# First loads of x and of the first weight chunk: one DMA queue before, two after

## The chip, the cores and the metric

The kernel runs on one core of one Trainium2 chip. The metric is the device time of one execution in microseconds (us); the median of three runs before the change is 1243.56 us (1243.49 to 1244.97). The core has TensorE (PE, matrix products), VectorE (DVE), ScalarE (ACT), GpSimd (POOL) and SyncE (SP, which only issues transfers and waits). Each engine executes its own instructions strictly in the order in which the program lists them; engines wait for one another, and for transfers, by semaphores.

## The reference

One inference step of a four-layer decoder trunk in float32 on 288 rows of x (256 of a prompt, 8 x 4 of samples), 1024 columns wide. Each layer computes `x += mixer(rmsnorm(x)); x += sqReLU-MLP(rmsnorm(x))`. Layer 0, in which all of the change lies, has the gating mixer:

```
u, v = split(gelu(h @ w_in), 2)          # h = rmsnorm(x); w_in is 1024 x 2048
v    = rmsnorm(v, sgu_g)
out  = (u * (masked w_s @ v + b_s)) @ w_out
```

## The kernel before

**Layout.** x is held transposed: eight tiles `x[k]` of 128 x 288. A weight matrix comes in chunks of 128 x 2048 (1 MB); a chunk of `w_in` gives two output tiles, each a sum over k = 0 to 7. Every product is made of three PE passes with operands split in two parts: whi * xh, whi * xl, wlo * xh (function `mm3`, lines 283 to 285). So a chunk is 2 x 8 x 3 = 48 matmuls.

**Splitting.** For each k ACT writes `xh[k]` (line 294) and DVE `xl[k]` (line 295). For each chunk ACT writes `whi` (line 207) and DVE `wlo` (line 208), in two halves; for the first chunk, raw0, in four quarters of 512 columns. Quarter s holds the weights of k = 2s and 2s+1, and the first two quarters are split in `W.piece()`, the other two in a second call; ahead of quarter s the source asks for `xh`, `xl` of k = 2s and 2s+1 (function `first` near the end of `body`). The raw buffers and the split buffers are three deep.

**The norm.** ACT squares x[k] (lines 300 and 306), POOL adds the squares (line 307, seven additions), a matmul sums them over partitions (line 321), ACT takes the root (line 329), and DVE makes 1/root with a Newton step (lines 330, 311 to 314). Only then can DVE scale the first chunk's result out of PSUM (line 481), and PE, which has five accumulators, gets one back for its sixth output tile. At the start PE runs 14 warm-up products (line 337) that need no data.

**What sets the order.** The source is not the order of execution. At build time a list scheduler orders each engine's instructions by its own estimates and priorities; the hardware then keeps that order. The lists shown under the change are from the built programs. Transfers use eight hardware semaphores in turn (DMAHW0 to 7): the ninth transfer waits, on its issuing engine, until the first has landed, and so on.

**The first loads.** All are issued by SP: aux (80 KB of small vectors), x[0], quarter 0, x[1..3], quarter 1, x[4..7], quarters 2 and 3, then chunks 1 and 2 in two halves each, `ident`, and the constants of layer 0.

Of the kernel before, what the change touches and what calls it, by code (L numbers as in the profile page):

```python
# [161 lines left out]
class Weights:  # L162
# [7 lines left out]
        self.todo = []  # L170
        self.first = None

    def load(self, upto, parts=None):
        while self.n_dma < min(upto, len(self.srcs)):
            i = self.n_dma
            if i not in self.raw:
                self.raw[i] = self.rawp.tile([P, 2048], F32, tag='raw', name=f'raw{i}')
                self.todo += [(i, p) for p in range(2)]
            t = self.raw[i]
            n = 4 if i < 1 else 2 if i < 3 else 1  # L180
            w = 2048 // n
            a, b = parts or (0, n)
            for s in range(a, b):
                self.nc.sync.dma_start(t[:, s * w:(s + 1) * w], self.srcs[i][:, s * w:(s + 1) * w])
            if b < n:
                return
            self.n_dma += 1

    def piece(self):
# [34 lines left out]
def body(tc, a, o, layers=(0, 1, 2, 3)):  # L224
    nc = tc.nc
    V, S, G, PE = nc.vector, nc.scalar, nc.gpsimd, nc.tensor
# [11 lines left out]
    W = Weights(tc, srcs, rawp, hip, lop)  # L238
# [3 lines left out]
    xall = persist.tile([P, KT, T], F32, name='x')  # L242
    x = [xall[:, k] for k in range(KT)]
    nc.sync.dma_start(aux, a['aux'])
    nc.sync.dma_start(xall[:, 0:1], a['xT'][:, 0:1])
    W.load(1, parts=(0, 1))
    nc.sync.dma_start(xall[:, 1:4], a['xT'][:, 1:4])
    W.load(1, parts=(1, 2))
    nc.sync.dma_start(xall[:, 4:8], a['xT'][:, 4:8])
    W.load(1, parts=(2, 4))  # L250
    A = {n: aux[:, i] for i, n in enumerate(AUX)}
    ident = persist.tile([P, P], F32, name='ident')
    ones = persist.tile([P, P], F32, name='ones')
# [952 lines left out]
def program(inputs, layers=(0, 1, 2, 3)):  # L1206
    import concourse.bacc as bacc
    nc = bacc.Bacc("TRN2", target_bir_lowering=False, num_devices=1)
    arrays, a, o = {}, {}, {}
    for n, v in layout(inputs).items():  # L1210
        arrays[f"in_{n}"] = v
        a[n] = nc.dram_tensor(f"in_{n}", v.shape, mybir.dt.from_np(v.dtype), kind="ExternalInput").ap()
    for n, s in OUTS.items():
        o[n] = nc.dram_tensor(f"out_{n}", s, F32, kind="ExternalOutput").ap()
    with tile.TileContext(nc) as tc:
        body(tc, a, o, layers)
    return nc, arrays
# [7 lines left out]
```

## Time and profile before

| | us |
|---|---|
| median of 3 runs | 1243.56 |
| the profiled execution's own time | 1242.8 |
| its span (first to last instruction) | 1241.1 |
| PE busy | 1216.4 (98%) |
| DVE busy | 853.4 (69%) |
| ACT busy | 679.2 (55%) |
| mean granted TensorE clock | 0.997 of full speed |

A row of the timeline gives the start in us from the span's start, the duration, the engine, the source line, the operation, out<-in, the count of merged instructions, and in brackets the idle time before it with what ended that. SPq rows are SP issuing transfers. In a table by windows each row is a stretch, with the busy time of each engine in it, the granted clock, the share of DMA engines that are busy, and GB/s.

### The profile page before, as it was taken

The page shows a single profiled execution, that of the slowest core. Times are in us where ns is not written, and L with a number is a line of the kernel's source. Part 1 is how long each engine was busy: PE and PEld are TensorE (multiplying, and loading weights), DVE is VectorE, ACT ScalarE, POOL GpSimd, SP SyncE. Part 2 cuts the span into 40 slices and gives each one's busy share as a digit, 9 for nine tenths or more (in the row PEclk, how much of TensorE's full clock was granted, in tenths as well). Part 3 has the DMA queues.
Part 4 walks back from the last instruction along what each step waited for, and adds up shares of the span by engine and source line. Part 5 has one row for each costly group of instructions (what it writes and reads, how often), then busy time and mean ns, then how long its engine had stood idle before and what let it go on. Part 6 is the DMA issues. An engine that isn't in the chain of part 4 may idle for free.

```text
span 1241.1 us, 23859 instructions
## 1 busy us (share of the span) xinstructions
PE 1216.4 (98%) x9802; PEld 1198.6 (97%) x9802; DVE 853.4 (69%) x1485; ACT 679.2 (55%) x1159; POOL 144.8 (12%) x192
## 2 busy tenths in 40 slices
PE   8999999999989999999999999999999999999997
PEld 7999999999889999999998999999999999999997
DVE  5789986676789976787698556555566686554553
ACT  5757734754686753574433457436645557634641
POOL 4302000001432200001111210000013110000011
PEclk9999999999999999999999999999999999999999
DMA  8537565565425786676677344444445535554431
GB/s 306 182 133 240 179 218 171 196 203 191 148 73 205 234 263 209 209 239 211 206 289 266 112 169 162 164 158 167 166 171 196 174 137 170 170 170 162 160 120 39
DMA packets 56006, 227.70 MB, mean 183 GB/s; under 512 B 16649, under 2 KB 22201, under 8 KB 33369
## 3 DMA queue, kind: packets, MB, share of 16 engines
q1 hardware_dynamic: 54472, 221.83, 53.2%
q0 software_dynamic: 848, 3.75, 0.9%
q8 instruction: 77, 1.26, 0.4%
q10 hardware_dynamic: 576, 0.59, 0.1%
q14 instruction: 33, 0.26, 0.1%
HBM read 209.45 MB, written 16.70 MB: 182 GB/s over the span
## 4 chain that ended last, share of the span: by engine, by line
PE 88%; DVE 7%; DMA 2%; POOL 1%; ACT 1%; issue 1%; SPq 0%; DVEq 0%; ACTq 0%
PE acc L285 27%; PE acc L283 27%; PE acc L284 27%; DVE wlo L208 2%; PE sec L1054 1%; PE sec L532 1%; PE acc L1092 1%; PE acc L1096 1%; PE acc L1046 1%; DMA sco<-scr 1%; DMA x<-in_xT 1%; DMA bt<-in_bt 0%; DVE hl L280 0%; POOL eg L666 0%; DVE xc L635 0%
## 5 line engine op out<-in xcount | busy, mean ns | idle before, releaser
L207 ACT ACTIVATE whi<-raw 128x1024 fp32r<-128x1024 f32 (+1 forms) x354 | 364.1, 1049 | 386.0 <-PE acc L284 364.4
L208 DVE TENSOR_TENSOR wlo<-raw,whi 128x1024 fp32r<-128x1024 f32 (+1 forms) x354 | 426.2, 1222 | 128.7 <-ACT whi L207 126.7
L283 PE MATMUL acc<-xh,whi 128*128 128x288 f32 x1472 | 440.4, 299 | 3.9 <-DVE t L481 1.8
L285 PE MATMUL acc<-xh,wlo 128*128 128x288 f32 x1472 | 437.9, 298 | 5.9 <-DVE wlo L208 5.8
L284 PE MATMUL acc<-xl,whi 128*128 128x288 f32 x1472 | 431.8, 294 | 0.0
L283 PE MATMUL acc<-hh,whi 128*128 128x288 f32 x1024 | 303.3, 296 | 0.0
L284 PE MATMUL acc<-hl,whi 128*128 128x288 f32 x1024 | 302.4, 295 | 0.7 <-DVE hl L280 0.7
L285 PE MATMUL acc<-hh,wlo 128*128 128x288 f32 x1024 | 301.5, 294 | 0.0
L283 PEld LDWEIGHTS acc<-xh,whi 128*128 128x128 f32 x1472 | 277.3, 188 | 7.9 <-ACT whi L207 2.7
L285 PEld LDWEIGHTS acc<-xh,wlo 128*128 128x128 f32 x1472 | 276.4, 188 | 8.0 <-DVE wlo L208 7.3
L284 PEld LDWEIGHTS acc<-xl,whi 128*128 128x128 f32 x1472 | 280.6, 191 | 1.6 <-DVE xl L295 0.3
L284 PEld LDWEIGHTS acc<-hl,whi 128*128 128x128 f32 x1024 | 192.4, 188 | 1.1 <-DVE hl L280 0.9
L285 PEld LDWEIGHTS acc<-hh,wlo 128*128 128x128 f32 x1024 | 192.7, 188 | 0.2 <-issue 0.2
L283 PEld LDWEIGHTS acc<-hh,whi 128*128 128x128 f32 x1024 | 192.2, 188 | 0.2 <-issue 0.2
L307 POOL TENSOR_TENSOR ss<-ss,sq 128x288 f32<-128x288 f32 x62 | 69.9, 1127 | 915.7 <-ACT sq L306 914.9
L433 DVE TENSOR_TENSOR t<-acc,r 128x288 f32<-128x288 f32 x64 | 29.3, 457 | 139.9 <-PE acc L285 139.9
L280 DVE TENSOR_TENSOR hl<-t,hh 128x288 fp32r<-128x288 f32 x128 | 57.5, 451 | 35.6 <-ACT hh L279 35.6
L410 ACT ACTIVATE t<-acc 128x288 f32<-128x288 f32 x128 | 51.4, 402 | 23.8 <-PE acc L285 23.7
L279 ACT ACTIVATE hh<-t 128x288 fp32r<-128x288 f32 x128 | 56.9, 444 | 3.7
L295 DVE SCALAR_TENSOR_TENSOR xl<-x,aux,xh 128x288 fp32r<-128x288 f32 x64 | 51.5, 815 | 10.2 <-ACT xh L294 10.2
L416 ACT ACTIVATE t<-t 128x288 f32<-128x288 f32 x128 | 56.0, 437 | 2.3 <-DVE hl L280 0.5
L294 ACT ACTIVATE xh<-x,aux 128x288 fp32r<-128x288 f32 x64 | 33.3, 527 | 28.9 <-DVE x L1113 15.3
(334 smaller groups left out, 1246.5 us busy)
## 6 DMA issues: line engine op xcount, KB each, us to landing
raw<-in_wall SPq DMA_DIRECT2D x173, 1024.0 KB, 5.0
sci<-scr SPq DMA_DIRECT2D x8, 768.0 KB, 8.7
sco<-scr SPq DMA_DIRECT2D x8, 768.0 KB, 7.3
scr<-zero SPq DMA_DIRECT2D x16, 256.0 KB
scr<-cn SPq DMA_DIRECT2D x8, 512.0 KB, 8.5
raw<-in_wall SPq DMA_DIRECT2D x4, 512.0 KB
bt<-in_bt SPq DMA_DIRECT2D x8, 256.0 KB
scr<-tab SPq DMA_DIRECT2D x8, 256.0 KB, 5.5
```

The lines of the kernel that those rows point to most:

```text
L207: nc.scalar.activation(h[:, c], self.raw[i][:, c], AF.Copy)
L208: nc.vector.tensor_tensor(l[:, c], self.raw[i][:, c], h[:, c].bitcast(F32), op=OP.subtract)
L279: S.activation(h, src, AF.Copy)
L280: V.tensor_tensor(l, src, h.bitcast(F32), op=OP.subtract)
L283: PE.matmul(ps, wh, h, start=first, stop=False)
L284: PE.matmul(ps, wh, l, start=False, stop=False)
L285: state['mm'] = PE.matmul(ps, wl, h, start=False, stop=last)
L294: state['xh'] = S.activation(xh[k], x[k], AF.Copy, scale=A[g][:, k:k + 1])
L295: V.scalar_tensor_tensor(xl[k], x[k], A[g][:, k:k + 1], xh[k].bitcast(F32), op0=OP.mult, op1=OP.subtract)
L307: G.tensor_tensor(state['ss'], state['ss'], q, op=OP.add)
L410: i = S.activation(q, ps[:, :T], AF.Relu)
L416: S.activation(q2, q, AF.Square)
```

## The change

x is loaded in five pieces on SP (x[0], x[1], x[2..3], x[4..5], x[6..7]) with no weights between them, and the four quarters of raw0 are issued by ACT on its own queue, ahead of everything else that ACT does.

```
-    def load(self, upto, parts=None):
+    def load(self, upto, eng=None):
...
-            a, b = parts or (0, n)
-            for s in range(a, b):
-                self.nc.sync.dma_start(t[:, s * w:(s + 1) * w], self.srcs[i][:, s * w:(s + 1) * w])
-            if b < n:
-                return
+            for s in range(n):
+                (eng or self.nc.sync).dma_start(t[:, s * w:(s + 1) * w], self.srcs[i][:, s * w:(s + 1) * w])
             self.n_dma += 1
...
     nc.sync.dma_start(aux, a['aux'])
-    nc.sync.dma_start(xall[:, 0:1], a['xT'][:, 0:1])
-    W.load(1, parts=(0, 1))
-    nc.sync.dma_start(xall[:, 1:4], a['xT'][:, 1:4])
-    W.load(1, parts=(1, 2))
-    nc.sync.dma_start(xall[:, 4:8], a['xT'][:, 4:8])
-    W.load(1, parts=(2, 4))
+    for b, e in ((0, 1), (1, 2), (2, 4), (4, 6), (6, 8)):
+        nc.sync.dma_start(xall[:, b:e], a['xT'][:, b:e])
+    W.load(1, eng=S)
```

The built program moves more than these loads. First SP, from its first transfer; x of 128x576 are the three pairs x[2..3], x[4..5], x[6..7], raw_131 is chunk 1, and [waits ...] names the semaphore of an earlier transfer that must have landed. After:

```order
L241 DMA aux<-in_aux 128x160
L243 DMA x<-in_xT 128x288 x2
L243 DMA x<-in_xT 128x576
L243 DMA x<-in_xT 128x576 [waits DMAHW0_49]
L243 DMA x<-in_xT 128x576 [waits DMAHW1_49]
L183 DMA raw_131<-in_wall 128x1024 [waits DMAHW2_49]
L183 DMA raw_131<-in_wall 128x1024 [waits DMAHW3_49]
```

DMAHW0 is the semaphore of quarter 0 on ACT's queue, DMAHW1 that of aux: SP now issues x[4..5] only when quarter 0 has landed. Before, no x load had such a wait.

Then ACT, from its first instruction to the last `xh`. Before (xh_91 to xh_98 are k = 0 to 7; whi_151 is the first chunk):

```order
L1177 ACT_TABLE_LOAD
L1177 ACTIVATE one_127<-eps 128x1
L294 ACTIVATE xh_91<-x,aux 128x288
L207 ACTIVATE whi_151<-raw_79 128x512
L294 ACTIVATE xh_92<-x,aux 128x288
L294 ACTIVATE xh_93<-x,aux 128x288
L294 ACTIVATE xh_94<-x,aux 128x288
L207 ACTIVATE whi_151<-raw_79 128x512
L294 ACTIVATE xh_95<-x,aux 128x288
L294 ACTIVATE xh_96<-x,aux 128x288
L207 ACTIVATE whi_151<-raw_79 128x512
```

After (xh_93 to xh_100 are k = 0 to 7; whi_153 is the first chunk):

```order
L183 DMA raw_83<-in_wall 128x512 x4
L1171 ACT_TABLE_LOAD
L1171 ACTIVATE one_129<-eps 128x1
L288 ACTIVATE xh_93<-x,aux 128x288
L288 ACTIVATE xh_97<-x,aux 128x288
L288 ACTIVATE xh_94<-x,aux 128x288
L288 ACTIVATE xh_98<-x,aux 128x288
L204 ACTIVATE whi_153<-raw_83 128x512 x2
L288 ACTIVATE xh_95<-x,aux 128x288
L288 ACTIVATE xh_99<-x,aux 128x288
L288 ACTIVATE xh_96<-x,aux 128x288
L288 ACTIVATE xh_100<-x,aux 128x288
```

ACT's order in k was 0, 1, 2, 3, ... with a quarter between; it is now 0, 4, 1, 5, two quarters, 2, 6, 3, 7. By the offsets of their operands in the built program the two quarters are the third (k = 4, 5) and then the first (k = 0, 1). DVE's `xl` and `wlo` follow the same order. PE's order in k is unchanged: 0, 1, 2, ... 7.

The next rows of ACT, up to the root of the norm (rq). After (sq are the squares of k = 2 and on; whi_238, whi_294, whi_401 are chunks 1, 2, 3):

```order
L300 ACTIVATE sq_184<-x 128x288
L204 ACTIVATE whi_153<-raw_83 128x512
L300 ACTIVATE sq_187<-x 128x288
L300 ACTIVATE sq_190<-x 128x288
L204 ACTIVATE whi_153<-raw_83 128x512
L300 ACTIVATE sq_193<-x 128x288
L300 ACTIVATE sq_196<-x 128x288
L204 ACTIVATE whi_238<-raw_131 128x1024
```

The two rows of whi_153 are the fourth quarter (k = 6, 7) and, last, the second (k = 2, 3). Before, only one quarter, the fourth, stood at this place, between sq_182 and sq_185; the second came before any square.

Last, DVE at the Newton step of the norm (r and rq), up to the first scalings of PSUM (t<-acc). Before:

```order
L330 TENSOR_SCALAR ms_352<-sec_350 128x288
L311 RECIPROCAL r_353<-rq_354 128x288
L312 SCALAR_TENSOR_TENSOR rq_354<-ms_352,r_353 128x288
L313 TENSOR_TENSOR rq_354<-rq_354,r_353 128x288
L314 SCALAR_TENSOR_TENSOR r_353<-rq_354,r_353 128x288
L481 TENSOR_TENSOR t_361<-acc_242,r_353 128x288
L481 TENSOR_TENSOR t_373<-acc_243,r_353 128x288
```

After (wlo_402 is chunk 3, wlo_486 chunk 4):

```order
L305 RECIPROCAL r_355<-rq_356 128x288
L205 TENSOR_TENSOR wlo_402<-raw_234,whi_401 128x1024
L306 SCALAR_TENSOR_TENSOR rq_356<-ms_354,r_355 128x288
L205 TENSOR_TENSOR wlo_486<-raw_236,whi_485 128x1024
L307 TENSOR_TENSOR rq_356<-rq_356,r_355 128x288
L205 TENSOR_TENSOR wlo_486<-raw_236,whi_485 128x1024
L308 SCALAR_TENSOR_TENSOR r_355<-rq_356,r_355 128x288
L475 TENSOR_TENSOR t_363<-acc_244,r_355 128x288
```

Three half-chunk splits of chunks 3 and 4 now stand inside the Newton step; before, they stood behind the scalings. ACT's halves of the same chunks stand, likewise, around rq and ahead of the table load for GELU. The first difference is at the start and the last one in the middle of layer 0's mixer; behind it the lists of all engines are the same.

## Rows read from the trace of the kernel before

**Rows 1.** The page: chain that ended last by engine; the commonest DMA issue.

```profile
PE 88%; DVE 7%; DMA 2%; POOL 1%; ACT 1%; issue 1%; SPq 0%; DVEq 0%; ACTq 0%
...
raw<-in_wall SPq DMA_DIRECT2D x173, 1024.0 KB, 5.0
```

**Rows 2.** Windows: stretch, length, busy PE, PEld, DVE, ACT, POOL, clock, DMA, GB/s.

```profile
0.00:40.00 40.00, 34.03 (x226) 30.87 (x227) 24.55 (x44) 25.51 (x50) 17.76 (x21) 1.00 0.71 250
40.00:1229.00 1189.00, 1178.79 (x9542) 1164.93 (x9542) 823.47 (x1427) 652.90 (x1109) 127.08 (x171) 1.00 0.54 182
```

**Rows 3.** Timeline of SP's queue: when each transfer is issued.

```profile
1.71 0.43 SPq L184 DMA_DIRECT2D raw<-in_wall  x1
...
9.53 0.33 SPq L454 DMA_DIRECT2D wT<-in_wsT  x1
10.20 0.34 SPq L456 DMA_DIRECT2D wS<-in_wsS  x1
10.85 0.35 SPq L459 DMA_DIRECT2D bsb<-in_bsr  x1
```

**Rows 4.** Timeline of ACT, 5 to 16 us.

```profile
5.43 0.63 ACT L207 ACTIVATE whi<-raw 128x512 fp32r<-128x512 f32 x1 [0.83 <-DMA raw<-in_wall]
...
8.79 0.62 ACT L207 ACTIVATE whi<-raw 128x512 fp32r<-128x512 f32 x1
9.54 0.97 ACT L294 ACTIVATE xh<-x,aux 128x288 fp32r<-128x288 f32 x2
10.41 0.62 ACT L207 ACTIVATE whi<-raw 128x512 fp32r<-128x512 f32 x1
10.93 0.95 ACT L294 ACTIVATE xh<-x,aux 128x288 fp32r<-128x288 f32 x2
11.78 0.43 ACT L300 ACTIVATE ss<-x 128x288 f32<-128x288 f32 x1
12.12 0.77 ACT L306 ACTIVATE sq<-x 128x288 f32<-128x288 f32 x2
...
14.82 0.44 ACT L306 ACTIVATE sq<-x 128x288 f32<-128x288 f32 x1 [0.91 <-POOL ss L307]
15.17 1.04 ACT L207 ACTIVATE whi<-raw 128x1024 fp32r<-128x1024 f32 x1
```

**Rows 5.** Timeline of POOL: the seven additions of squares.

```profile
12.63 9.15 POOL L307 TENSOR_TENSOR ss<-ss,sq 128x288 f32<-128x288 f32 x7 [10.46 <-ACT sq L306]
```

**Rows 6.** Timeline of PE, 0 to 30 us.

```profile
1.13 4.76 PE L337 MATMUL sec<-ones 128*128 128x128 f32 x28 [1.13 <-DVE eps L256]
6.11 0.41 PE L283 MATMUL acc<-xh,whi 128*128 128x288 f32 x1 [0.22 <-ACT whi L207]
...
23.23 0.30 PE L283 MATMUL acc<-xh,whi 128*128 128x288 f32 x1
...
23.62 0.65 PE L321 MATMUL sec<-ss,ones 128*128 128x288 f32 x2
...
29.26 0.40 PE L283 MATMUL acc<-xh,whi 128*128 128x288 f32 x1 [1.82 <-DVE t L481]
```

**Rows 7.** Timeline of DVE and ACT at the norm, and a later half split.

```profile
24.31 0.50 ACT L329 ACTIVATE rq<-sec,eps 128x288 f32<-128x288 f32 x1 [3.66 <-PE sec L321]
...
24.84 0.46 DVE L330 TENSOR_SCALAR ms<-sec 128x288 f32<-128x288 f32 x1 [1.98 <-ACT rq L329]
...
34.05 1.22 DVE L208 TENSOR_TENSOR wlo<-raw,whi 128x1024 fp32r<-128x1024 f32 x1 [0.49 <-ACT whi L207]
```

**Rows 8.** PE around its longest idle time, in layer 1.

```profile
355.73 0.61 PE L285 MATMUL acc<-xh,wlo 128*128 128x288 f32 x1 [3.78 <-DVE wlo L208]
356.13 0.45 PE L283 MATMUL acc<-xh,whi 128*128 128x288 f32 x1
...
359.01 0.31 PE L283 MATMUL acc<-xh,whi 128*128 128x288 f32 x1
```

**Rows 9.** Window behind that idle time (columns as in rows 2).

```profile
357.00:358.00 1.00, 1.00 (x6) 1.00 (x5) 1.00 (x2) 1.00 (x2) 0.00 (x0) 0.50 0.33 123
```

## The prediction, put on record before the changed kernel ran

> **What bounds the kernel now.** I read the page's busy times and its chain first. PE is busy 98% of the span (the table above) and holds 88% of the chain [rows 1]: a change is worth what it does to PE's idle time. The windows say where that is [rows 2]: in the first 40 us PE is idle for 40.00 - 34.03 = 5.97 us, in the next 1189 us for 10.21 us. All that the change moves lies in the first 40 us.
>
> Next, the timeline of SP's queue, which gives landing times, since SP waits for an earlier transfer before it issues a later one [rows 3]: x[4..7] has landed at 9.5, quarter 2 (counting from 0) at 10.2, quarter 3 at 10.85 us. With the sizes in the queue's order (aux 80 KB, x[0] 144, quarter 256, x[1..3] 432, quarter 256, x[4..7] 576, two quarters of 256) that is a curve: 1744 KB at 9.5, 2000 at 10.2, 2256 at 10.85. Quarter 0 (480 KB) ends ACT's idle time at 5.43 [rows 4].
>
> Then ACT and PE side by side. ACT splits quarter 0 at 5.43 and PE starts at 6.11, just behind it; quarter 1 is split at 8.79 to 9.41 [rows 4, 6]. PE reaches the sum of the norm at 23.62 and, after its sixth output tile has waited for a PSUM bank, goes on at 29.26 [rows 6]. From there PE hardly waits. So two moments measure the start: 23.62 and 29.26.
>
> **The change, part by part.**
>
> *Issue.* Four issues move from SP to ACT, ahead of ACT's table load. One costs about 0.43 us on SP [rows 3]; at that price ACT is busy for 1.7 us longer. That lies wholly ahead of the wait below, which ends at 10.0, and costs nothing.
>
> *When x[4..5] lands.* This now counts because the order puts xh of k = 4 second in ACT's strict queue: everything ACT does, the first quarter included, stands behind it. x[4..5] is itself issued only when quarter 0 has landed. On SP's queue 656 KB stand ahead of it, and with its own 288 KB that makes 944 KB; ACT's queue brings 1024 KB beside them. No row here shows two loading queues at once, so I bound it. If SP's queue wins, 944 KB and quarter 0 have moved, 1200 KB, at 7.7 us (on the line from 480 KB at 5.4 to 1744 KB at 9.5); but then quarter 2, which ACT splits first, comes late. Both are needed, 944 + 768 = 1712 KB, so one of the two is not there before 9.4. If everything comes at once it is 10.85, and with one more issue 11.3. With equal shares 1888 to 1968 KB have moved, 10.0 us. I take 10.0, which is also near the rows for the same data.
>
> [...]
>
> *ACT's new order.* By rows 4, an xh takes 0.43 us (9.54 to 10.41 for two), a quarter 0.52 to the next instruction and 0.62 to its end, a square 0.34. From 10.0: xh of k = 4, 1, 5 (that of k = 0 is done earlier), quarter 2 at 11.3, quarter 0 at 11.8, ready at 12.4: PE starts at 12.5 instead of 6.11. Then xh of k = 2, 6, 3, 7 from 12.3, the first square at 14.05, the next at 14.4. The squares alternate between two buffers, so they wait for POOL. Before, POOL's first addition began 0.51 us after the start of the second square (12.12 to 12.63), and the square that waits for POOL came 2.19 us later, at 14.82 [rows 4, 5]. Now: 14.4 + 0.51 + 2.19 = 17.1 for the last square ahead of quarter 1, quarter 1 at 17.45, ready at 18.07. Quarter 3 fits in between. PE wants quarter 1 (k = 2 and 3) directly after quarter 0; with 12 of 48 matmuls done it stands until 18.1.
>
> *PE up to the sum of the norm.* From 18.1 there are 36 matmuls of the first chunk and 48 of the second, at 0.13 us (three in 23.23 to 23.62) [rows 6]: 10.9 us, and 0.3 for the wlo of quarter 1. Chunk 1's splits are done by about 22 to 24 and don't stop it, as they did before. The sum comes at 29.3, 5.7 later than 23.62.
>
> *The Newton step.* Before, rq began 0.69 after the sum, ms 0.53 after that, and PE went on 4.42 after ms [rows 6, 7]. Now three half splits of wlo stand among DVE's Newton instructions, 1.22 us each [rows 7]: 3.66 us. Their inputs are there: chunk 3 is issued when the last wlo of the first chunk is done, about 19, chunk 4 by about 24, and 1 MB lands 5.0 us after its issue [rows 1]. ACT's three halves and the table load end near 35 and lie beside this. So PE goes on at 29.3 + 0.69 + 0.53 + 4.42 + 3.66 = 38.6, against 29.26: 9.3 us later. What stalls longer than before is the sixth output tile, from 32.7 to 38.6.
>
> *What comes back.* Chunks 3 and 4 are split earlier, so DVE and ACT have less to do from 39 on. PE, though, had almost no idle time to give back there [rows 2]; I put it at nothing.
>
> *The clock.* [...] PE will now be idle from 5.9, the end of the warm-up products [rows 6], to 12.5, from about 14.5 to 18.1, and from 32.7 to 38.6. [...] I count 1.2 for the second, since 0.3 us of waiting covers part of it, and 1.0 for the third, where PE soon waits for GELU anyway: 2.2 us.
>
> **Sum.** 9.3 + 2.2 = 11.5 us. On the profiled execution's 1242.8 that is 1254.3; the median of the runs is 0.8 above that execution, so 1255.1.
>
> **The rivals.** A kernel within 0.2% (2.5 us) of before can't be told from no change.
>
> - *The clock stays up* (chance 0.16): the three idle times are not answered by the lower level. Against it speaks the 3.78 us of rows 8; for it, that the 1.82 us of rows 6 went unpunished and that work lies between the first two stretches. 1242.8 + 9.3 + 0.8 = 1252.9.
> - *The loads come better than by equal shares* (0.12): both x[4..5] and quarter 2 by 9.4, with quarter 2 last, which ACT then begins at 9.4 in place of 11.3: 1.9 us less, 1253.2.
> - *They come worse* (0.09): x[4..5] at 11.3, all else 1.3 later: 1256.4.
> - *The late start is given back later* (0.03, the other side): layer 1 and 2 hold most of the 10.21 us of PE's idle time behind 40 us [rows 2]. Were those waits for something that does not start later, such as work already ahead of PE, the delay would fill them: 1255.1 - 10.2 = 1244.9, no change. It decides from the point where DVE and ACT run ahead of PE by 3.8 us or more ahead of layer 1's waits. Against it: the orders there are the same, and the longest wait is for a DVE split, and DVE gets its work from PE's results.
> - *The order is no hindrance and the loads are simply earlier* (0.03): quarter 0 is no longer issued behind aux and x[0], which ended at 1.71 [rows 3], two issues of some 0.45 us each, so PE starts 0.9 us earlier: 1242.7 at 1243.6 for before, no change; with all of the 5.97 us of idle time in the first 40 us gone, 1237.6. ACT's queue and the wait on SP speak against it, since xh of k = 4 can't come before 7.7.
>
> [...]
>
> **How the numbers follow.** My forecast, 1255.1, has a chance of 0.57. The first two rivals reach down to 1252.9, and together, clock and loads, to 1251.0; the third to 1256.4, and with both clock terms at 1.4 to 1257.0. The range is 1251.0 to 1257.5. Slower by over 0.2% are all of these, 0.94; same 0.04; faster 0.02.
>
> **What would show it.** Right: PE's first matmul on real data near 12.5; a second idle time that ends near 18.1 with quarter 1's split; the sum of the norm near 30; the sixth tile's matmul with an idle time of some 6 us ahead of it, near 40; granted clock of 0.50 in stretches behind these. Wrong: a first matmul before 9, an ACT row of k = 4 that does not wait for its load, no split between DVE's Newton rows, or PE idle time behind 45 us that shrinks by several us.

## The result, and the profile after

The changed kernel takes 1253.8 us, median of 6 runs (1252.88 to 1254.97), against 1243.53 (1243.03 to 1244.97, 6 runs) beside it: ratio 1.0079 (95% interval 1.0068 to 1.0090), 10.3 us slower. Forecast were 1255.1 and a range of 1251.0 to 1257.5. The profiled execution took 1253.64 us, its span is 1251.9; before, 1242.8 and 1241.1.

The windows of the changed kernel, columns as in [rows 2]:

```profile
0.00:40.00 40.00, 27.31 (x151) 26.11 (x151) 22.97 (x34) 19.82 (x33) 12.24 (x17) 0.79 0.75 263
40.00:1229.00 1189.00, 1179.08 (x9534) 1164.69 (x9535) 825.47 (x1435) 656.93 (x1121) 127.75 (x173) 1.00 0.55 182
```

Behind 40 us PE is idle for 9.92 us, 10.21 before. The loss lies ahead: by 40 us PE has done 151 matmuls in place of 226, and its mean clock there is 0.79.

ACT's timeline at the start (start, duration, engine, line, operation; in brackets the idle time before it and what ended that), which answers to [rows 4]:

```profile
0.81 1.87 ACTq L183 DMA_DIRECT2D raw<-in_wall  x4
...
9.04 1.39 ACT L288 ACTIVATE xh<-x,aux 128x288 fp32r<-128x288 f32 x3 [2.94 <-DMA x<-in_xT]
10.34 1.13 ACT L204 ACTIVATE whi<-raw 128x512 fp32r<-128x512 f32 x2
...
16.10 0.44 ACT L300 ACTIVATE sq<-x 128x288 f32<-128x288 f32 x1 [0.91 <-POOL ss L301]
16.45 0.61 ACT L204 ACTIVATE whi<-raw 128x512 fp32r<-128x512 f32 x1
```

ACT stands until 9.04 for xh of k = 4. Quarters 2 and 0 come behind it in one row, and quarter 1, at 8.79 before, only at 16.45, behind a square that waits for POOL.

PE of the same execution, which answers to [rows 6]:

```profile
11.52 0.61 PE L277 MATMUL acc<-xh,whi 128*128 128x288 f32 x1 [4.52 <-ACT whi L204]
...
17.12 0.61 PE L277 MATMUL acc<-xh,whi 128*128 128x288 f32 x1 [2.35 <-ACT whi L204]
...
31.35 0.65 PE L315 MATMUL sec<-ss,ones 128*128 128x288 f32 x2
...
39.88 0.61 PE L277 MATMUL acc<-xh,whi 128*128 128x288 f32 x1 [4.69 <-DVE t L475]
```

Its first matmul on real data comes at 11.52 in place of 6.11, the sum of the norm at 31.35 in place of 23.62 (7.73 later), and PE goes on at 39.88 in place of 29.26 (10.62 later). DVE between the two last, which answers to [rows 7]:

```profile
32.57 0.46 DVE L324 TENSOR_SCALAR ms<-sec 128x288 f32<-128x288 f32 x1 [5.18 <-ACT rq L323]
32.94 1.94 DVE L305 RECIPROCAL r<-rq 128x288 f32<-128x288 f32 x1
34.80 1.16 DVE L205 TENSOR_TENSOR wlo<-raw,whi 128x1024 fp32r<-128x1024 f32 x1
35.88 0.45 DVE L306 SCALAR_TENSOR_TENSOR rq<-ms,r 128x288 f32<-128x288 f32 x1
36.24 1.22 DVE L205 TENSOR_TENSOR wlo<-raw,whi 128x1024 fp32r<-128x1024 f32 x1
37.38 0.45 DVE L307 TENSOR_TENSOR rq<-rq,r 128x288 f32<-128x288 f32 x1
37.75 1.22 DVE L205 TENSOR_TENSOR wlo<-raw,whi 128x1024 fp32r<-128x1024 f32 x1
38.88 0.46 DVE L308 SCALAR_TENSOR_TENSOR r<-rq,r 128x288 f32<-128x288 f32 x1
39.37 1.79 DVE L475 TENSOR_TENSOR t<-acc,r 128x288 f32<-128x288 f32 x4
```

The three half splits stand between the Newton instructions, none of which waits for anything but its turn. Last, the clock (third column from the end), which answers to [rows 9]:

```profile
11.00:23.00 12.00, 9.13 (x35) 8.46 (x36) 8.69 (x11) 10.02 (x19) 8.61 (x8) 0.50 0.97 360
23.00:24.00 1.00, 1.00 (x8) 1.00 (x8) 1.00 (x1) 0.00 (x0) 1.00 (x2) 0.78 0.62 98
...
42.00:43.00 1.00, 1.00 (x7) 0.88 (x5) 0.00 (x0) 0.39 (x2) 0.22 (x1) 0.50 1.04 442
```

PE's granted clock is 0.50 from its first matmul on real data until 23.4, and again for 4.0 us from 39.88 on.

When the loads land, from SP's queue, which answers to [rows 3]: it waits for quarter 2 before the first of these issues, and for quarter 3 before the second.

```profile
8.66 0.67 SPq L1173 DMA_DIRECT2D ident<-in_ident  x1
9.38 0.59 SPq L448 DMA_DIRECT2D wT<-in_wsT  x1
```

With x[4..5] there at 9.04 (ACT, above), 1968 KB have landed by 9.4; before it was 2000 KB at 10.2. On the line of [rows 3], 1968 KB belong to 10.1, so the bytes are there 0.7 earlier. Landing times differ between traces, but not by so much that this is lost: 1968 KB are there at 9.4 to 9.5 in the four traces with the new loads that show it, and at 10.1 to 10.8 in the four with the old ones.

### The profile page after: what moved, and what is told of

It reads as the page before. It is cut to its first block, busy times and chain, and to the rows that moved or that the text cites. A ratio compares the mean times of both kernels' runs of the same rounds, so it can differ in the third digit from the quotient of the medians.

```text
span 1251.9 us, 23861 instructions
## 1 busy us (share of the span) xinstructions
PE 1221.0 (98%) x9802; PEld 1204.5 (96%) x9802; DVE 854.8 (68%) x1485; ACT 679.5 (54%) x1159; POOL 141.6 (11%) x192
## 3 DMA queue, kind: packets, MB, share of 16 engines
HBM read 209.45 MB, written 16.70 MB: 181 GB/s over the span
## 4 chain that ended last, share of the span: by engine, by line
PE 88%; DVE 8%; POOL 1%; ACT 1%; DMA 1%; issue 1%; DVEq 0%; ACTq 0%
PE acc L279 27%; PE acc L277 27%; PE acc L278 27%; DVE wlo L205 2%; PE sec L1048 1%; PE acc L1086 1%; PE acc L1040 1%; PE sec L526 1%; PE acc L1090 1%; DVE hl L274 0%; POOL eg L660 0%; PE sec L487 0%; DVE xc L629 0%; PE sec L945 0%; ACT whi L204 0%
```

## The experiments

Theory A: the order that the list scheduler made of the new loads costs the time, the loads themselves nothing. Theory B: the loads on two queues cost a part themselves, for instance since x[0] lands later. Ratios are to runs of the kernel before beside each group of experiments, with 95% intervals. The new loads are a second queue and also x in five pieces in place of three; no run here separates these two.

**1. The new loads, the old order.** The start is written out in the order of the kernel before, each instruction of ACT and DVE chained to the one ahead of it (n = square, q = quarter, x = xh and xl):

```
-    W.piece()
-    W.piece()
-    with tc.issue_after(state['xh'].ins):
-        for k in range(KT):
-            norm_square(k)
+    order = 'x0 q0 x1 x2 x3 q1 x4 x5 q2 x6 x7 n0 n1 n2 q3 n3 n4 n5 n6 n7'.split()
+    for o_ in order:
...
```

> The loads of the changed kernel (x in five pieces on SP, quarters on ACT's queue), but ACT and DVE forced into the order of before at the start: k = 0, quarter 0, k = 1, 2, 3, quarter 1, k = 4, 5, quarter 2, k = 6, 7, three squares, quarter 3. The build puts no half split into the Newton step then. Theory A (the static order costs, not the loads): the first real matmul near 6.5 us, the sum of the norm near 23.5, time 1243.5, at most 1245. Rival B (two queues bring x and the quarters too late, whatever the order): x[4..5] still lands at 9.0 and the rest of the start stays behind it, time 1249 or more.

1248.97 us (1248.19 to 1249.98), ratio 1.0040 (1.0026 to 1.0055): by the time alone, theory B. The trace says otherwise. ACT's rows from quarter 2 on stand where they stood before, to 0.02 us (10.41; first half of chunk 1 at 15.18, before 15.17). But the scheduler had moved two other things: the sum of the norm forward into chunk 1, where PE waited 4.47 us for POOL at 23.82, and what is seen under experiment 5. The run did not isolate the loads.

**2. The old loads, the new order.** Same edit on the kernel before, with the changed kernel's order:

```
+    order = 'x0 x4 x1 x5 q2 q0 x2 x6 x3 x7 n0 n1 n2 q3 n3 n4 q1 n5 n6 n7'.split()
```

> The loads of the kernel before, all on SP, but ACT and DVE forced into the changed kernel's order at the start (k = 0, 4, 1, 5, quarters 2, 0, k = 2, 6, 3, 7, three squares, quarter 3, two squares, quarter 1); the build then gives the changed kernel's order everywhere else too, the three half splits inside the Newton step included. Theory A: x[4..7] lands at 9.5 instead of x[4..5] at 9.0, so all is half a us later than in the changed kernel: 1254.3. Rival B: near before, 1245.

1256.47 us (1256.03 to 1257.67), ratio 1.0099 (1.0084 to 1.0115). The build put four half splits into the Newton step, not three as I had written. The order alone costs more than the whole change: xh of k = 4 waits until 10.21, the first matmul comes at 12.70, PE goes on at 41.16. Given this order, xh of k = 4 starts 1.17 us earlier with the loads on two queues. Not all of that is the loads': x[4..7] landed 0.67 later in this trace (10.20) than in the trace of the kernel before (9.53), which has the same loads. And the fourth split, at about 1 us (experiments 3 and 6), is part of what the time is above that of the changed kernel.

**3. The changed kernel with the splits of chunks 3 and 4 behind the Newton step.**

```
+                if i in (3, 4):
+                    for j in self.after:
+                        stay.enter_context(self.tc.issue_after(j.ins))
```

Here `after` holds the last Newton instruction and the first two scalings.

> The changed kernel, with the half splits of chunks 3 and 4 forced on DVE behind the Newton step and the first two scalings; the order at the start is the changed kernel's. Theory A: the three splits, 1.2 us each, leave the path to the sixth output tile, PE goes on near 36.3 instead of 39.9, and its idle time shrinks from 4.7 to about 1.2 us, after which the clock need not fall: 1253.8 - 3.6 - 1.1 = 1249.1. If the splits only fill time in which DVE would wait anyway, 1253.8 stays; if they come back as a wait later (GELU and scalings behind them), 1251 to 1253.

1249.51 us (1248.92 to 1250.28), ratio 1.0042 (1.0027 to 1.0057), 4.3 less than the changed kernel (4.6 by the ratios to the runs beside each), as expected. DVE and PE of this run:

```profile
32.24 0.46 DVE L329 TENSOR_SCALAR ms<-sec 128x288 f32<-128x288 f32 x1 [5.99 <-ACT rq L328]
32.61 1.94 DVE L310 RECIPROCAL r<-rq 128x288 f32<-128x288 f32 x1
34.59 0.46 DVE L311 SCALAR_TENSOR_TENSOR rq<-ms,r 128x288 f32<-128x288 f32 x1
35.08 0.46 DVE L312 TENSOR_TENSOR rq<-rq,r 128x288 f32<-128x288 f32 x1
35.58 0.46 DVE L313 SCALAR_TENSOR_TENSOR r<-rq,r 128x288 f32<-128x288 f32 x1
36.14 0.82 DVE L481 TENSOR_TENSOR t<-acc,r 128x288 f32<-128x288 f32 x2
```

```profile
36.65 0.40 PE L282 MATMUL acc<-xh,whi 128*128 128x288 f32 x1 [1.79 <-DVE t L481]
```

From ms to t it takes 3.90 us, in the changed kernel 6.80: the three splits cost 2.90, or 0.97 each, not their duration of 1.16 to 1.22. A split starts 0.1 before the row ahead of it ends, and so does the Newton row behind it; two Newton rows that follow each other directly have a gap of 0.03 to 0.10. And PE, having waited 1.79, has its full clock behind the wait (1.00 from 36 to 38 us).

**4. The changed kernel with more products of ones**: 25 warm-up products in place of 14, and 9 ahead of quarter 1's first matmul.

```
-    warm_up(14)
+    warm_up(25)
...
+                n = {(0, 2, 0): 9}.get((c, k, m), 0) if late else 0
```

> The changed kernel with 25 instead of 14 warm-up products at the start and 9 more behind the products of k = 0 and 1, so that PE is not idle while it waits for quarter 0 and for quarter 1. Clock theory: the 84 matmuls behind quarter 1 run at 0.13 us instead of 0.24 for the first 26 of them, the sum of the norm comes at 28.5 instead of 31.35, time 1253.8 - 2.8 = 1251.0. If the clock does not matter to the path, 1253.8; if the added products end after the data have come, 1254 to 1255.

1252.67 us (1252.02 to 1253.17), ratio 1.0067 (1.0052 to 1.0082). The clock is 1.00 until 38 us. From quarter 1's first matmul to the sum of the norm it now takes 12.01 us (17.61 to 29.62), in the changed kernel 14.23: 2.2 us of it were the low clock. In these 12.01 PE stands 0.51 for the wlo of quarter 1 (at 18.91), a wait that the low clock had covered. PE goes on 1.73 earlier (38.15), with the low clock still behind it (0.50 from 39 to 41). At the first addition of the next norm 2.00 are gained, at POOL's last addition 1.23, and the median is 1.1 less; the intervals of the two ratios overlap, so a gain in time is not shown. It is less than expected (see experiment 11).

**5. Experiment 1 with the sum of the norm held behind chunk 1, and the splits of chunk 3 held behind the first two scalings.**

```
             if c == late and before:
-                before()
+                with tc.issue_after(state['mm'].ins):
+                    before()
```

> The two-queue loads of the changed kernel, with the start written in the order of the kernel before on ACT, DVE and PE: the squares' sum stays PE's 113th row behind the whole of chunk 1, and chunk 3 is split behind the first two scalings, so that no split stands in the Newton step. Theory A (only the order that the build sets costs time, the loads nothing): first matmul on real data near 6.8, sum of the norm at 23.6 to 24.0, PE goes on at 29.3 to 29.7, 1243.5 us, between 1242.8 and 1244.5. Theory B (the loads on two queues cost part of the 10 us themselves, and the 5 us of the first experiment were theirs): sum at 25 or later, 1247 us or more.

1247.59 us (1245.81 to 1248.64), ratio 1.0027 (1.0016 to 1.0038). Again not what theory A expects; the cause shows in PE's row ahead of chunk 1 and the windows behind:

```profile
18.50 0.61 PE L282 MATMUL acc<-xh,whi 128*128 128x288 f32 x1 [2.50 <-ACT whi L209]
```

```profile
18.00:19.00 1.00, 0.50 (x2) 0.50 (x3) 0.63 (x2) 0.65 (x2) 0.92 (x2) 0.50 1.01 387
24.00:25.00 1.00, 1.00 (x7) 1.00 (x7) 0.00 (x0) 0.00 (x0) 0.67 (x2) 0.62 0.99 401
```

The first half split of chunk 1 on ACT ends at 16.70, the second at 18.45 (17.41 + 1.04): PE waited for the second. The built program tells why. The half whose load signals DMAHW2 is the one PE needs first:

```
21 L209 ACTIVATE whi1_238<-raw1_131 128x1024 [waits DMAHW3_49]
24 L209 ACTIVATE whi1_238<-raw1_131 128x1024 [waits DMAHW2_49]
```

The scheduler had swapped the two halves. Experiments 1, 5 and 6 have this, and experiment 8 has it in chunk 2; the kernels before and after do not have it in chunk 1. The wait of 2.50 us (0.75 before) brought the low clock, from 18.5 until 24.8.

**6. Experiment 5 without holding the splits back**: the build then puts four half splits into the Newton step.

> As the kernel with the order held, except that four half splits of 1.16 us each stand between DVE's Newton instructions (one more than in the changed kernel) and the start is undisturbed. Theory A: the sum of the norm stays at 23.6 to 24.0, PE goes on 4 x 1.16 = 4.6 later, at 34.1 in place of 29.4, with a low clock of about 1.0 behind it: 5.6 us above the kernel with the order held, 1249.1 us. If the splits were covered by PE's work on other tiles (a rival), within 1 us of it. Theory B makes no difference here beyond its own offset.

1250.80 us (1250.62 to 1252.03), ratio 1.0061 (1.0048 to 1.0075), 3.2 more than experiment 5 where 5.6 were expected. From the sum to PE's going on it is 9.55 us (26.84 to 36.39) against 5.63: 3.92 for four splits, again 0.98 each. The times are closer than that since experiment 5's own sum came 1.17 later (28.01), and its clock fell behind the wait too (0.50 from 36 to 38).

**7. The old loads in a better order**: quarter 3 split ahead of the squares, the first half of chunk 1 ahead of the fourth. The sum of the norm is held behind chunk 1, as in experiment 5.

```
+    order = 'x0 q0 x1 x2 x3 q1 x4 x5 q2 x6 x7 q3'.split()
```

> Loads of the kernel before; ACT splits quarter 3 ahead of the first square and the first half of chunk 1 ahead of the fourth square. PE's waits of 0.75 and 0.62 us ahead of chunk 1 should go, 1.4 us, if POOL's additions, which end about 0.45 later than 21.78, are still done when PE comes to the sum at 22.2: 1242.2 us, between 1241.5 and 1243.5. If POOL now ends last, 1243.0.

1242.77 us (1240.73 to 1244.26, 11 runs), ratio 0.9991 (0.9982 to 1.0000). PE goes on at 27.61 in place of 29.26, but its clock behind the same wait (1.81 us, before 1.82) is the low one here (0.50 from 28 to 31): of 1.65 us 0.15 is left at the first addition of the next norm (84.08 against 84.23), and 0.60 at POOL's last addition. The interval of the ratio reaches up to no gain.

**8. The new loads in that order.**

> The better order of the kernel beside it with the two-queue loads, chunk 3 split on DVE between the second and third scaling. Theory A: the same as that kernel within 0.5 us, 1242.5 us, since the loads are not what PE waits for once the order is the same. Theory B: above it by 3 us or more.

1243.12 us (1242.05 to 1245.02, 11 runs), ratio 0.9996 (0.9987 to 1.0004): no difference to experiment 7 that can be told. The build slipped something in again: on POOL two mask operations among the squares' additions (rows under experiment 10), so that PE waited 2.11 us for POOL ahead of the sum.

**9. Experiment 5 with the halves of chunks 1 and 2 held in order.**

```
+                if p and i in (1, 2):
+                    for j in self.prev[i]:
+                        stay.enter_context(self.tc.issue_after(j.ins))
```

> The kernel of the fifth run (two-queue loads, start written in the order of the kernel before), in which the build had put the second half of chunk 1 ahead of the first on ACT, so that PE waited for both; here the halves of chunks 1 and 2 are held in order. Theory A (order alone): PE begins chunk 1 near 16.8 after an idle time of about 0.8 in place of 2.5, the clock stays at 1.00, sum of the norm near 24.1, PE goes on near 29.8, 1244.0 us (1243.0 to 1245.0). Theory B (the loads cost part of it): the 2.5 us wait or another one stays, 1247 us.

1243.63 us (1242.60 to 1246.75, 11 runs), ratio 0.9999 (0.9990 to 1.0008). PE of this run (rows between those shown are left out), beside [rows 6]:

```profile
6.91 0.40 PE L287 MATMUL acc<-xh,whi 128*128 128x288 f32 x1 [0.79 <-ACT whi L1215]
16.21 0.40 PE L287 MATMUL acc<-xh,whi 128*128 128x288 f32 x1 [0.75 <-ACT whi L213]
23.82 0.75 PE L325 MATMUL sec<-ss,ones 128*128 128x288 f32 x2
29.56 0.40 PE L287 MATMUL acc<-xh,whi 128*128 128x288 f32 x1 [1.81 <-DVE t L487]
```

PE starts 0.80 later than before, the sum of the norm is 0.20 later, and the time is that of the kernel before. This is nearly the loads alone; besides them only the splits of chunk 3 are held, as in experiment 5. Within the interval, 1.2 us less to 1.0 more, the loads cost nothing and bring nothing. Theory B falls as an account of the 10.3 us.

**10. Experiment 8 with the halves held likewise.**

> The two-queue loads with the better start order, and the halves of chunks 1 and 2 held in order (in the eighth run those of chunk 2 were swapped). PE no longer waits for both halves of chunk 2; its wait for POOL ahead of the sum of the norm (2.11 us there) hides part of that: 1242.8 us (1242.0 to 1243.5); if POOL alone sets the sum, 1243.1 as there.

1243.36 us (1243.27 to 1244.41, 11 runs), ratio 0.9995 (0.9986 to 1.0003). POOL alone still sets the sum, for which PE waits 2.11 us at 24.34. Its last rows:

```profile
19.31 1.09 POOL L466 TENSOR_SCALAR_AFFINE_SELECT wT<-wT 128x1024 f32<-128x1024 f32 x1
20.37 1.77 POOL L307 TENSOR_TENSOR ss<-ss,sq 128x288 f32<-128x288 f32 x1
22.10 1.43 POOL L467 TENSOR_SCALAR_AFFINE_SELECT wS<-wS 32x256 f32<-32x256 f32 x1
23.50 0.78 POOL L307 TENSOR_TENSOR ss<-ss,sq 128x288 f32<-128x288 f32 x1
```

In experiment 7 the seven additions stand together, and end at 21.8.

**11. Experiments 3 and 4 together.**

> The changed kernel's start order, with the Newton splits moved behind it and 25 + 9 warm-up products that keep the clock up, both edits of the third and fourth run together. If the three terms (start order, Newton splits, clock) add: 1249.5 less the 1.7 us by which the fourth run went on earlier, 1247.8 us, and no stretch at clock 0.50 behind 37 us; what is then left above the kernel before, some 4 us, is the start order by itself. If the clock term is bound up with the splits (the fall behind them), 1249 or more.

1249.90 us (1249.59 to 1251.11), ratio 1.0049 (1.0034 to 1.0065): a miss, no less than experiment 3. The mechanism did what it should: clock 1.00 from 10 to 46 us, the sum at 29.46 and PE on at 35.09, both 1.56 earlier than in experiment 3. At POOL's last addition 0.2 of that is left. About 0.6 went between 107 and 278 us, where PE had no more idle time but took longer, and 0.8 between 620 and 710, where this execution has a wait of 0.55 us for a small transfer that the other lacks. Why is open; in other runs the same stretches vary by as much. The last 0.7 went at the very end, where PE's last eight products took 1.98 us here and 1.24 in experiment 3, behind the same wait of 2.02 (see the first point of the last section). So the gain of the warm-up is shown at the start of the program, and not in its time.

**12. Experiment 7 with its clock kept up**: five products of ones, into unused columns of the fifth tile's bank, in the wait for the Newton step.

```
+                    if late and (c, k, m) == (2, 0, 1):
+                        with tc.issue_after(state['mm'].ins), tc.high_priority(offset=0):
+                            for _ in range(5):
+                                i = PE.matmul(ps[0][:, 384:], ones, ones, start=True, stop=True)
+                        stay.enter_context(tc.issue_after(i.ins))
```

> The seventh run's kernel (loads of before, better start order) with five products of ones, written to unused columns of the fifth tile's bank, in PE's wait for the Newton step. There PE went on at 27.61, 1.65 before the kernel before did at 29.26, but the clock then stood at 0.50 until about 31 and 12 matmuls cost 0.24 each, so that only 0.6 us were left at the end. If the clock term is what took the gain: no stretch at 0.50 behind 27.6, PE goes on at 27.6 to 27.8, and the end comes 1.3 us earlier than in the seventh run: 1241.5 us, 0.998 of before. If the products themselves hold PE up or the gain is lost elsewhere: 1242.8, as there.

1241.66 us (1240.47 to 1242.26, 11 runs), ratio 0.9982 (0.9973 to 0.9991): 1.9 us less than the kernel before beside it. Against experiment 7 the median is 1.1 less, but the intervals overlap; there the gain is shown by the traces, where the first addition of the next norm comes 1.52 earlier (82.56 against 84.08). Windows of experiment 7, and then of this one, with its PE rows:

```profile
28.00:29.00 1.00, 1.00 (x7) 1.00 (x6) 0.82 (x2) 0.72 (x3) 0.00 (x0) 0.50 0.40 164
29.00:30.00 1.00, 1.00 (x6) 1.00 (x5) 0.00 (x0) 0.00 (x0) 0.00 (x0) 0.50 0.00 0
```

```profile
28.00:29.00 1.00, 1.00 (x9) 1.00 (x10) 0.85 (x3) 0.94 (x3) 0.00 (x0) 1.00 0.18 74
29.00:30.00 1.00, 1.00 (x10) 0.99 (x9) 0.09 (x1) 0.00 (x0) 0.00 (x0) 1.00 0.06 25
```

```profile
25.85 1.28 PE L371 MATMUL acc<-ones 128*128 128x128 f32 x10
27.82 0.40 PE L283 MATMUL acc<-xh,whi 128*128 128x288 f32 x1 [0.69 <-DVE t L488]
```

Behind the wait PE does 9 to 10 matmuls in a microsecond where it did 6 to 7.

## Why the prediction was right, step by step

The mechanism was the one forecast, and the runs separate its two parts. From the changed kernel to experiment 3 (no splits in the Newton step) it is 4.3 us, from there to experiment 9 (old start order too, loads as changed) 5.9, and experiment 9 is the kernel before within 0.1%. The groups of runs had somewhat different times of the kernel before; by the ratios to these the parts are 4.6 and 5.3. Single terms were off, and partly cancelled:

- *When x[4..5] lands.* Forecast 10.0, measured 9.04. SP and ACT share as assumed: 944 KB on SP's queue are there at 9.04, all 1024 KB on ACT's by 9.4. What I had too small is the rate of both together: 1968 KB by 9.4, against 2000 KB at 10.2 [rows 3]. That is the condition of the rival "the loads come better": x[4..5] at 9.04, quarter 2 by 8.66. Only half of its 1.9 us came, since ACT began quarter 2 at 10.34 and not at 9.4, behind three xh; the measured time lies between that rival's 1253.2 and the forecast. All that follows is 1.0 earlier: first matmul 11.52 (forecast 12.5), quarter 1 at 17.12 (18.1).
- *ACT's order.* Both terms as forecast: xh of k = 4 holds everything behind it, and quarter 1 stands behind a square that waits for POOL.
- *From quarter 1 to the sum of the norm.* Forecast 11.2 and 1.2 of clock, measured 14.23. **This clock term is the one that was mis-sized.** I had taken the length of the low stretch from [rows 8, 9], 12 matmuls at 0.24 in place of 0.13 and the one ahead of them: 13 x 0.11 = 1.4. That as much would follow here was my estimate, and no run shows the 1.2. What the runs show in its place is a stretch at a clock of 0.50 of 26 matmuls, from 17.12 to 23.39, at 0.24 in place of 0.13: 2.9 us by this count. What it cost is what experiment 4 gets back, 2.2: at full clock the same stretch takes 12.01, not 11.2, among other things because PE then stands 0.51 for the wlo of quarter 1, where I had 0.3.
- *The Newton step.* Forecast 9.3 from the sum to PE's going on, measured 8.53, with 4.69 of idle time ahead of it in place of some 6. The three splits cost 2.90 and not 3.66; experiments 3, 2 and 6 agree on 0.97 to 0.98 for each.
- *The clock behind it.* Forecast 1.0, my estimate from the same rows; no run shows it by itself. What the runs show in its place is 1.06: an early landmark behind the start, the first addition of the next norm on POOL, is 11.68 later than before, and at PE's going on it was 10.62. The two rows, before and after:

```profile
84.23 0.80 POOL L307 TENSOR_TENSOR ss<-ss,sq 128x288 f32<-128x288 f32 x1 [27.68 <-ACT sq L306]
```

```profile
95.91 0.80 POOL L301 TENSOR_TENSOR ss<-ss,sq 128x288 f32<-128x288 f32 x1 [27.68 <-ACT sq L300]
```

- *What comes back.* Nothing was forecast. The last such addition is 10.85 later, so 0.83 of the 11.68 came back, 0.62 of it by 271 us. The stretch from 102 to 271 takes 168.2 to 169.4 us in the fourteen traces (before 169.0), so I don't call it an effect of the change.

By terms: 5.7 - 1.0 + 3.0 (2.2 of clock, 0.8 of rest) gives the 7.7 at the sum; 2.9 for the splits and 1.1 behind them make 11.7, against 11.5. The two terms that were too large (loads 1.0, splits 0.8) covered the 1.8 that the stretch to the sum lacked (14.23 against 12.4): that the total was nearer than its parts is luck. How much of the 10.3 us in the program's time is the clock's stays open: at landmarks of the start the traces show what it takes, but experiments 4 and 11, which keep it up, are not clearly faster than the changed kernel and experiment 3.

## What to carry to other kernels

Where a scheduler orders the instructions, a change of the first loads is a change of every engine's order: read the built order, not the diff, before you say what the loads do. An experiment that holds the order must hold all of it; here a moved sum, two swapped halves and two mask operations each made a run look like an effect of the loads. And once a tensor engine is the bound, price an idle time by what its clock does behind it, too.

## What the runs showed of the hardware

- *The same wait, two clocks.* PE waited 1.79 to 1.82 us for the Newton step in eight of the traces. Before, and in experiments 3 and 8 to 11, it kept its clock (1.00); in experiments 5 and 7 it fell to 0.50 behind the wait. The order of the instructions alone doesn't decide it. At the program's end PE waits 2.02 us in all fourteen traces and then does the same eight products, in 1.11 to 1.98 us; before, and in experiment 11:

```profile
1233.72 1.11 PE L353 MATMUL acc<-r,ident 128*128 128x72 f32 x8 [2.02 <-DVE r L314]
1240.02 1.98 PE L352 MATMUL acc<-r,ident 128*128 128x72 f32 x8 [2.02 <-DVE r L313]
```

  The granted clock behind it was 1.00 and 0.50. Executions of one kernel differ too: of the 11 of experiment 9, the five with a mean clock of 0.995 or 0.996 took 1242.60 to 1243.25 us, the six with 0.993 or 0.994 took 1243.63 to 1246.75. So one trace for a kernel can't tell what its clock does behind a wait of this length; what decides is open.
- *The low stretch has no fixed length.* Counted from PE's going on: 3.3 us of work after an idle time of 3.78 (355.73 to 359.01 in [rows 8]); 4.0 after 4.69 (changed kernel at 39.88); 3.4 after 1.81 (experiment 7, where it begins at 28.0, 0.4 behind PE's going on); 6.3 after 2.35 (changed kernel at 17.12, the clock already low) and 6.3 after 2.50 (experiment 5).
- *Two queues at once.* x[0] comes later: ACT's first xh starts at 5.57 to 6.18 in the ten traces with two queues, at 3.73 to 4.06 in the four with one. Quarter 0, the first on ACT's queue, comes earlier: SP issues x[4..5], which waits for it, at 4.88 in the changed kernel and 4.51 in experiment 9, where before it ended ACT's wait at 5.43. The last pieces come earlier (1968 KB by 9.4 to 9.5, against 10.1 to 10.8). Whether the second queue does this or the finer pieces of x is not tested.
- *A short operation between two dependent ones*, here a half split in the Newton step, cost 0.97 to 0.98 us (experiments 3 and 6) where its row says 1.16 to 1.22.
